# Two blocks less to fetch in each opening: sums added onto raw blocks that are kept

## The chip, the cores and the metric

The kernel runs on 1 core of one Trainium2 chip. The time is the device time of one execution in microseconds. Of the core's engines the text speaks of PE (matmuls; PEld loads its weights), DVE (element-wise arithmetic), ACT (copies, casts, functions), POOL (GpSimd) and SP; here POOL and SP mostly start transfers. Each engine works through its own list of instructions in order.

## The reference

A trunk of two layers over 528 frames (16 meta tokens and 512 inputs) of width 1024, in float32:

```
h = h + 0.5 * swiglu(rmsnorm(h, g1), w_gate1, w_up1, w_down1)      # width 2816
u = rmsnorm(h, gm);  q, k, v, a, b, g_sb, g_conv = split(u @ w_in)
h = h + (sigmoid(g_sb) * attention(q, k, v) @ w_attn_out
         + sigmoid(g_conv) * conv(a, b) @ w_conv_out) @ w_out
h = h + 0.5 * swiglu(rmsnorm(h, g2), w_gate2, w_up2, w_down2)
```

with `swiglu(x, G, U, W) = (silu(x @ G) * (x @ U)) @ W`. The conv branch begins with `a * sigmoid(b)`, so a and b form pairs of products as G and U do. A final norm closes the trunk.

## The kernel before

The weights come from memory in float32. Every block of weights (128 x 1024) is split into a high part `wh` (a cast, on ACT, L80) and a low part `wl` (the block less its high part, on DVE, L81); so are the activations (`uh`, `ul`). A product is then three matmuls: high by high, high by low, low by high. Such a prepared block is called ready.

The products of two blocks of output columns with two halves of the tokens are formed by Strassen's scheme in Winograd's form with seven instead of eight products. What lies behind a pair of column blocks (G and U at the same columns, or b and a) is: blocks `w11`, `w12`, `w21`, `w22`, and sums of them: `s1` = w11 + w12 (in the signs in which the blocks are stored), `s2` = s1 + w22, `s3` = w22 + w12, and `s4` = s1 + w21. Sums with w12 are made in flight: SP loads one block into a tile, and then POOL starts a second transfer of w12 that accumulates onto it. The other two sums are made by DVE (s2 at L283; s4 at L505, `add_w21`, in an opening). The sums of the activations have the names `sh` and `sl`.

**Openings.** At the start of a mixer's projection of a and b, and of each FFN but the first, the first two pairs of columns are worked on together, so that PE has work while the norm's scale and the activation sums are still being made. There are five openings: mixer of layer 0, second FFN of layer 0, first FFN of layer 1, mixer of layer 1, second FFN of layer 1. `OPENING` (L115) is their order of 14 units; the number is the pair (0 is called the first pair below, 1 the second). `o11` and `o21` are the blocks w11 and w21 by the unsummed activations. `w22`, `s3`, `s4` and `s2` follow with the sums of activations as these become ready.

**Preparing.** `unit` (L294) hands a ready block to PE and has the units that follow prepared two ahead in an opening (`LOOK - 1`). `prep_unit` (L254) casts, makes the low part and the DVE sums. A priority for DVE's and ACT's evictions of PE's results (`opposite`, L478; `kept`, L465) puts them ahead, and `follow` keeps a preparation behind them. All instructions of a list are then in the order in which the program was scheduled; a load that needs a tile which is still in use waits at the head of SP's list, and all loads behind it wait too.

**Tiles.** Raw blocks (`wr`, three tiles, `fetch`, L212) are taken in the order of `fetches`; `drop` gives one back. Sums in flight have tiles of their own: `s1` (two tiles) and `s3` (two in an FFN, one in the mixer); `fetch_sums` (L233) takes the next ones from the list `later_sums`. In an opening before the change:

- o11 of both pairs, o21 of both, s1 of the first pair, w22 of both: raw tiles. o11's raw block is given back when it has been split, and w11 is loaded again for s1.
- w21 of both pairs, s1 of the second pair: the `s1` tiles. o21's raw block is given back too, and w21 is loaded again.
- `WHEN` (L117) says at which units how many sums are fetched.
- o21 of the first pair has its low part made on POOL's queue (L268): ACT writes the negative high part, and a transfer adds the block.

In a quad of the main part (not an opening) the sums come as w11 (a raw block) and s1, and `DONE` (L119) says what is given back after which unit; the change does not touch it.

Of the kernel before, what the change touches and what calls it, by code (L numbers as in the profile page):

```python
# [7 lines left out]
F32 = mybir.dt.float32  # L8
# [3 lines left out]
ALU = mybir.AluOpType  # L12

P = 128
# [4 lines left out]
HALF = T // 2  # L19
# [42 lines left out]
def kernel(ctx, tc, hT, par, const, wg1, wu1, wd1, win, wao, wco, wout, wg2, wu2, wd2, out):  # L62
    nc = tc.nc
    act, dve, pool, pe = nc.scalar, nc.vector, nc.gpsimd, nc.tensor
# [32 lines left out]
    def fn(out, in_, func, **kw):  # L97
        need = SETS[func]
        if table["set"] != need:
            load = act.preload_act_table_set(need)  # L100
            for p in table["acts"]:
# [9 lines left out]
    QUAD = ("w11", "s1", "s2", "w21", "s3", "w22", "s4")  # L111
    RAW_OF = {"w11": (0, 0), "w22": (1, 1), "w12": (0, 1), "w21": (1, 0),
              "o11": (0, 0), "o21": (1, 0)}
    OPEN = ("o11", "o21")
    OPENING = (("o11", 0), ("o11", 1), ("o21", 0), ("s1", 0), ("s2", 0), ("o21", 1), ("w22", 0), ("s3", 0), ("s1", 1),  # L115
               ("s2", 1), ("s4", 0), ("s3", 1), ("w22", 1), ("s4", 1))
    WHEN = {("s2", "s1"): 1, ("s3", "w22"): 1, ("s4", "s2"): 1, ("s4", "w22"): 2}  # L117
    BLOCKS = QUAD + OPEN
    DONE = {"w11": ("w11",), "s1": (), "s2": (), "w21": (), "s3": ("s3",), "w22": ("w22",), "s4": ("s1", "w21")}  # L119

# [17 lines left out]
    units, opened = [], set()  # L138
# [36 lines left out]
    ready, raws, counted = {}, {}, set()  # L175
    quads = {"pool": None, "of": None}

    def pieces(n, block=None):

        key, src, nk = units[n]  # L180
        if nk in BLOCKS:
            wg, wu, m = src
            k, c = RAW_OF[block or nk]
            return [(4 * e, 4 * e + 4, w[m + c, :, 4 * k:4 * k + 4]) for e, w in enumerate((wg, wu))]
        return [(0, nk, src[:, :nk])]
# [4 lines left out]
    for n, (key, src, nk) in enumerate(units):  # L190
        at = key[1:]
        if nk == "w11":
            later_sums += [(n, "s1"), (n, "s3")]
            fetches += [(n, (name, *at), name) for name in ("w11", "w22", "w21")]
        elif at in opened and nk in QUAD:
            if nk == "s1" and units[n - 1][2] in OPEN:
                later_sums += [(n, "s3"), (n, "w21")]
                fetches.append((n, key, nk))
            elif nk == "s1":
                later_sums += [(n, "s1"), (n, "s3"), (n, "w21")]  # L200
            elif nk == "s2":
                fetches.append((n, ("w22", *at), "w22"))
        elif nk not in QUAD:
            fetches.append((n, key, nk))

    def load(raw, n, *blocks):
# [5 lines left out]
    def fetch(spare=None):  # L212

        while state["fetch"] < len(fetches) and (spare or state["out"] < RAW):
            n, key, block = fetches[state["fetch"]]
            state["fetch"] += 1
            if spare:
                raw = spare
            else:
                state["out"] += 1  # L220
                counted.add(key)
                raw = wpool.tile([P, 8, P], F32, tag="wr", bufs=RAW, name="wr")
            load(raw, n, *(("w11", "w12") if block == "s1" else (block,)))
            raws[key] = raw
            if spare:
                return

    def drop(key):

        del raws[key]  # L230
        state["out"] -= key in counted

    def fetch_sums(count):  # L233

        some = []
        for n, name in later_sums[state["sums"]:state["sums"] + count]:
            if units[n][0][1:3] == quads["of"]:
                some.append((n, name))
        state["sums"] += len(some)
        for n, name in some[::-1]:  # L240
            tag = "s3" if name == "s3" else "s1"
            bufs = 1 if name == "s3" and units[n][0][1] == 2 else 2
            raws[(name, *units[n][0][1:])] = quads["space"].tile([P, 8, P], F32, tag=tag, bufs=bufs, name=tag)
        for n, name in some:
            load(raws[(name, *units[n][0][1:])], n, *{"s1": ("w11", "w12"), "s3": ("w22", "w12")}.get(name, (name,)))
# [8 lines left out]
    def prep_unit():  # L254
        n = state["prep"]
        key, src, nk = units[n]
        state["prep"] += 1
        fetch()
        hi = wpool.tile([P, 8, P], F32R, tag="wh", bufs=4, name="wh")
        lo = wpool.tile([P, 8, P], F32R, tag="wl", bufs=4, name="wl")  # L260
        ready[key] = (hi, lo)
        if nk not in QUAD:
            raw, nk0, nk = raws[key], nk, 8 if nk in OPEN else nk
            if key[0] in MIXER and key[0] + str(key[2]) not in ("q0", "k0") or nk0 == "o21" and units[n - 1][2] == "o11":
                act.copy(hi[:, :nk], raw[:, :nk])  # L265
                act.activation(lo[:, :nk], raw[:, :nk], AF.Copy, scale=-1.0)
                for a, b, src in pieces(n):
                    pool.dma_start(lo[:, a:b], src.bitcast(F32R), accum_op=ALU.add)  # L268
            else:
                pair_ = split(raw[:, :nk], hi[:, :nk], lo[:, :nk])  # L270
                if state["behind"]:
                    for i, engine in zip(pair_, ("act", "dve")):
                        follow(i, engine)
            drop(key)
        else:
            at = key[1:]
            if at in opened:
                fetch_sums(WHEN.get((nk, units[n - 1][2]), 0))
            elif nk == "w11":
                fetch_sums(2)  # L280
            if nk == "s2" or nk == "s4" and at not in opened:
                x, y = raws[("s1", *at)], raws[("w22" if nk == "s2" else "w21", *at)]
                i = dve.tensor_tensor(out=x, in0=x, in1=y, op=ALU.add)  # L283
                if at in opened:
                    follow(i, "dve")
            pair_ = split(raws[("s1" if nk in ("s2", "s4") else nk, *at)], hi, lo)
            if at in opened:
                for i, engine in zip(pair_, ("act", "dve")):
                    follow(i, engine)
            for d in DONE[nk]:  # L290
                drop((d, *at))
        fetch()

    def unit(*key):  # L294
# [146 lines left out]
    def pair(ptile, sp, st, mode, of, ats, between, take, done):  # L441
# [56 lines left out]
        between(ptile(), copy)  # L498

        Bs.append(kept(As[1], False))  # L500
        G, q, E, c22 = {}, {}, {}, {}

        def add_w21(n):
            x, y = raws[("s1", *of, ats[n])], raws[("w21", *of, ats[n])]
            dve.tensor_tensor(out=x, in0=x, in1=y, op=ALU.add)  # L505

        def step(name, n):
            if (name, n) in (("w22", 0), ("s4", 0)):
                add_w21(int(name == "s4"))
            w = unit(name, *of, ats[n])  # L510
            if name == "o21":
                products(As[n], w, x(0, 1))
                (out if n else take)(n, As[n], 0, 0)
                if n:
                    keep, Bs[n], G[n] = Bs[n], ptile("pe"), ptile()
                    begin(Bs[n], keep)
            elif name == "s1":
                if not n:
                    G[n] = ptile()
                products(G[n], w, sx(0), True)  # L520
                q[n] = kept(G[n])
            elif name == "s2":
                products(Bs[n], w, sx(1))
                E[n] = ptile()
                opposite(E[n], Bs[n], q[n])
            elif name == "s3":
                products(Bs[n], w, sx(2))
                c22[n] = sp.tile([P, 2, TH], F32, tag="c22", bufs=2, name="c22")
                opposite(c22[n], Bs[n], q[n])
                take(n, c22[n], 1, 1)  # L530
            elif name == "w22":
                products(E[n], w, sx(3))
                out(n, E[n], 1, 0)
            else:
                done(n, 1)
                products(Bs[n], w, x(1, 1))
                out(n, Bs[n], 0, 1)
                done(n, 0)
# [95 lines left out]
    def ffn(l, fi, st, mode, after):  # L634
# [3 lines left out]
        with tc.tile_pool(name=f"ffn{l}{fi}", bufs=1, reuse_waits="tile") as fp, \  # L638
# [215 lines left out]
            with tc.tile_pool(name=f"quad{l}{fi}", bufs=1, reuse_waits="tile") as sp:  # L854
                quads.update(pool=sp, space=sp, of=(fi, l))
                if not first:
                    fetch_sums(2)
                (first_head if first else head)()
                m = PLAIN_FIRST
                for gi, (m0, m1) in enumerate(GROUPS):  # L860
                    while m < m1:
                        quad(sp, m)
                        m += 2
                    if gi < len(GROUPS) - 1:
                        down(gi, gi == 0 and not first)
                quads["pool"] = None
# [7 lines left out]
    def mixer(l, st, omode, after):  # L874
        last = omode == XO
        with ExitStack() as es:
# [73 lines left out]
            with tc.tile_pool(name=f"glu{l}", bufs=1, reuse_waits="tile") as glu, \  # L950
# [33 lines left out]
                quads.update(pool=glu, space=gls, of=(2, l))  # L984
                if l == 0:
                    constants(gls)
                fetch_sums(2)
                with tc.manual_schedule(engines={mybir.EngineType.PE}):
                    pair(btile, glu, st, FULL, (2, l), (0, 2), between, take, done)
                quads["pool"] = None  # L990
# [382 lines left out]
```

## Time and profile before

| | us |
|---|---|
| median of 3 runs | 2134.2 (2132.87 to 2135.08) |
| the profiled execution's own time | 2139.23 |
| span of its trace | 2137.5 |
| PE busy | 2116.6 (99%) |
| DVE busy | 1595.7 (75%) |
| ACT busy | 1170.3 (55%) |
| POOL busy | 513.2 (24%) |
| moved by DMA | 333.29 MB |

The five openings lie at about 365 to 412, 722 to 770, 1078 to 1126, 1434 to 1482 and 1778 to 1826 us of the span. A row of the timeline gives start, length, engine, line, operation, the tile written, the tiles read and, in brackets, how long the engine stood idle before it and who released it. `wr` is a raw tile, `s` an s1 or s3 tile. SPq and POOLq are the engines' issuing of transfers. In the chain of waits a row `DMA wr<-wu` runs from the issue of a transfer to its landing. A block of an FFN is two transfers of 256 KB: one from `wg` (gate) and one from `wu` (up).

### The profile page before, as it was taken

The numbers are of one execution on the slowest core, as the hardware profiler recorded it, in microseconds if no ns is written. First come the engines' busy times: TensorE is split into PE (matmuls) and PEld (weight loads), VectorE is DVE, ScalarE is ACT, GpSimd is POOL, SyncE is SP. The second block draws the span as 40 slices with busy tenths as digits, with TensorE's granted clock in tenths as the row PEclk, the third lists the DMA queues.
The fourth block names the chain that finished last, engine by engine and source line by source line (L and its number), as shares of the span: only waits on it lengthen the run. The fifth ranks groups of instructions, "written<-read, shape, count | busy, mean of one in ns | idle before, by whom it ended". The sixth has DMA issues, their size and how long they took to land.

```text
span 2137.5 us, 39987 instructions
## 1 busy us (share of the span) xinstructions
PE 2116.6 (99%) x16058; PEld 2031.3 (95%) x16058; DVE 1595.7 (75%) x2230; ACT 1170.3 (55%) x1663; POOL 513.2 (24%) x475
## 2 busy tenths in 40 slices
PE   9999999999999999999999999999999999999998
PEld 9999999999999999999999999999888888999897
DVE  6867688788876777577787676887788767867685
ACT  5434356577776645343564343565778775444354
POOL 1322321311111141313123223213212112422320
PEclk9999999999999999999999999999999999999999
DMA  7465538555578867464386655375656788765542
GB/s 228 136 167 142 144 104 229 160 135 123 128 174 178 198 175 185 120 167 119 99 204 173 167 145 142 104 223 155 143 123 140 182 186 200 186 178 143 144 109 79
DMA packets 151833, 333.29 MB, mean 156 GB/s; under 512 B 16864, under 2 KB 21088, under 8 KB 151648
## 3 DMA queue, kind: packets, MB, share of 16 engines
q1 hardware_dynamic: 110928, 235.27, 34.7%
q0 software_dynamic: 40032, 94.91, 26.2%
q8 instruction: 126, 2.06, 0.4%
q14 instruction: 59, 0.48, 0.1%
q10 hardware_dynamic: 688, 0.55, 0.1%
HBM read 324.25 MB, written 6.42 MB: 155 GB/s over the span
## 4 chain that ended last, share of the span: by engine, by line
PE 91%; DVE 4%; DMA 3%; ACT 1%; issue 1%; SPq 0%; DVEq 0%; POOL 0%; ACTq 0%; POOLq 0%
PE pb L771 15%; PE ps L771 15%; PE ps L916 13%; PE ps L311 12%; PE ps L902 10%; PE pe L311 6%; PE pb L311 5%; PE pe L771 5%; DMA wr<-wu 1%; PE z L1101 1%; DMA s<-wg 1%; PE po L1145 1%; DVE wl L81 1%; PE z L1124 1%; PE pe L462 1%; PE be L462 1%
## 5 line engine op out<-in xcount | busy, mean ns | idle before, releaser
L80 ACT CAST wh<-wr 128x1024 fp32r<-128x1024 f32 (+4 forms) x298 | 265.6, 900 | 331.4 <-PE ps L311 85.5
L81 DVE TENSOR_TENSOR wl<-wr,wh 128x1024 fp32r<-128x1024 f32 (+4 forms) x298 | 331.6, 1117 | 57.9 <-ACT wh L80 55.6
L80 ACT CAST wh<-s 128x1024 fp32r<-128x1024 f32 x171 | 179.1, 1049 | 271.6 <-DVE s L283 94.1
L81 DVE TENSOR_TENSOR wl<-s,wh 128x1024 fp32r<-128x1024 f32 x171 | 233.0, 1362 | 55.1 <-ACT wh L80 54.4
L829 POOL TENSOR_TENSOR h<-h,dt 128x528 f32<-128x528 f32 (+1 forms) x96 | 177.3, 1855 | 247.4 <-DVE dt L827 247.3
L916 PE MATMUL ps<-uh,wh 128*128 128x264 f32 (+1 forms) x664 | 207.5, 312 | 0.0
L916 PE MATMUL ps<-ul,wh 128*128 128x264 f32 (+1 forms) x664 | 203.6, 307 | 0.0
L916 PE MATMUL ps<-uh,wl 128*128 128x264 f32 (+1 forms) x664 | 203.5, 307 | 0.0
L210 POOL DMA_DIRECT2D s<-wg x81 | 71.6, 884 | 523.5 <-DMA s<-wg 290.8
L945 DVE SCALAR_TENSOR_TENSOR y<-uc,prm,y 128x528 f32<-128x528 f32 (+1 forms) x240 | 184.5, 807 | 0.5
L771 PE MATMUL ps<-ul,wh 128*128 128x264 f32 (+1 forms) x576 | 163.7, 284 | 0.0
L771 PE MATMUL pb<-sl,wh 128*128 128x264 f32 (+1 forms) x576 | 163.3, 283 | 0.0
L771 PE MATMUL ps<-uh,wl 128*128 128x264 f32 (+1 forms) x576 | 163.3, 283 | 0.0
L771 PE MATMUL pb<-sh,wl 128*128 128x264 f32 (+1 forms) x576 | 163.2, 283 | 0.0
L771 PE MATMUL pb<-sh,wh 128*128 128x264 f32 (+1 forms) x576 | 162.9, 283 | 0.0
L771 PE MATMUL ps<-uh,wh 128*128 128x264 f32 (+1 forms) x576 | 162.6, 282 | 0.0
L311 PE MATMUL ps<-ah,wh 128*128 128x264 f32 (+1 forms) x616 | 141.9, 300 | 0.0
L311 PE MATMUL ps<-al,wh 128*128 128x264 f32 (+1 forms) x616 | 141.8, 300 | 0.0
L311 PE MATMUL ps<-ah,wl 128*128 128x264 f32 (+1 forms) x616 | 141.7, 300 | 0.0
L265 ACT CAST wh<-wr 128x1024 fp32r<-128x1024 f32 x89 | 93.4, 1049 | 82.0 <-PE ps L916 28.3
L916 PEld LDWEIGHTS ps<-uh,wl 128*128 128x128 f32 x664 | 125.0, 188 | 5.9
L916 PEld LDWEIGHTS ps<-uh,wh 128*128 128x128 f32 x664 | 124.9, 188 | 5.4
(419 smaller groups left out, 6833.4 us busy)
## 6 DMA issues: line engine op xcount, KB each, us to landing
wr<-wd SPq DMA_DIRECT2D x96, 384.0 KB, 3.8
wr<-wg SPq DMA_DIRECT2D x129, 256.0 KB, 3.1
wr<-wu SPq DMA_DIRECT2D x129, 256.0 KB, 3.7
wr<-win SPq DMA_DIRECT2D x56, 512.0 KB, 3.8
wl<-win POOLq DMA_DIRECT2D x52, 512.0 KB, 7.8
s<-wg SPq DMA_DIRECT2D x87, 256.0 KB, 4.8
s<-wu SPq DMA_DIRECT2D x87, 256.0 KB, 5.6
s<-wg POOLq DMA_DIRECT2D x81, 256.0 KB, 5.5
```

What stands on the lines that cost most here:

```text
L80: i = act.copy(hi, x)
L81: return i, dve.tensor_tensor(out=lo, in0=x, in1=f(hi), op=ALU.subtract)
L210: queue.dma_start(raw[:, a:b], src, **kw)
L265: act.copy(hi[:, :nk], raw[:, :nk])
L311: pe.matmul(ps[:, c, :n], wt[:, k0 + k, :], xt[:, s:s + n], start=(k == 0 and pi == 0), stop=(k == end and pi == 2))
L462: pe.matmul(ps[:, e, :TH], wt[:, 4 * e + kk, :], xt, start=start and kk == 0 and pi == 0, stop=kk == KH - 1 and pi == 2, skip_group_check= ...
L771: pe.matmul(ps[:, e, :TH], wt[:, 4 * e + kk, :], xt, start=start and kk == 0 and pi == 0, stop=kk == 3 and pi == 2, skip_group_check=True)
L829: pool.tensor_tensor(out=tri(h[j], mode), in0=tri(h[j], mode), in1=tri(t, mode), op=ALU.add)
L902: pe.matmul(ps, wt[:, k0 + k, :], xt[:, s], start=(n == 0 and pi == 0), stop=(n == nk - 1 and pi == 2))
L916: pe.matmul(ps, wt[:, k, :], xt[:, s], start=(n == 0 and pi == 0), stop=(n == KD - 1 and pi == 2))
L945: t = dve.scalar_tensor_tensor(out=y, in0=uc[i][:, c0 + k:k + T], scalar=col(w0 + k), in1=y, op0=ALU.mult, op1=ALU.add)
L1101: pe.matmul(z[:, hh, :n], kk[r, ks], qq[r, q0:q0 + n], start=(pi == 0), stop=False, skip_group_check=True)
```

## The change

In an opening, o11's raw tile is kept: POOL adds w12 onto it, once it has been split, and it becomes s1. o21's raw block is kept until s4's sum. So w11 and w21 are loaded once instead of twice for each pair. s1 of both pairs now are in raw tiles, with w21 of the first pair in the third; w21 of the second pair and both blocks w22 are in the `s1` tiles. `fetch_sums(3)` loads the second pair's o21, the first's w22 and the first's s3 at the start, and one each follows after s3 and w22. The first pair's s3 is worked on ahead of its w22 instead of behind it. `c22`, the result of s3, gets its two tiles at the start. `WHEN` is gone.

```diff
-    OPENING = (("o11", 0), ("o11", 1), ("o21", 0), ("s1", 0), ("s2", 0), ("o21", 1), ("w22", 0), ("s3", 0), ("s1", 1),
+    OPENING = (("o11", 0), ("o11", 1), ("o21", 0), ("s1", 0), ("s2", 0), ("o21", 1), ("s3", 0), ("w22", 0), ("s1", 1),
                ("s2", 1), ("s4", 0), ("s3", 1), ("w22", 1), ("s4", 1))
-    WHEN = {("s2", "s1"): 1, ("s3", "w22"): 1, ("s4", "s2"): 1, ("s4", "w22"): 2}
...
         elif at in opened and nk in QUAD:
-            if nk == "s1" and units[n - 1][2] in OPEN:
-                later_sums += [(n, "s3"), (n, "w21")]
-                fetches.append((n, key, nk))
-            elif nk == "s1":
-                later_sums += [(n, "s1"), (n, "s3"), (n, "w21")]
-            elif nk == "s2":
-                fetches.append((n, ("w22", *at), "w22"))
-        elif nk not in QUAD:
+            if nk == "s3" and units[n - 1][2] == "o21":
+                later_sums += [(n - 1, "o21"), (n + 1, "w22"), (n, "s3")]
+            elif nk == "s3":
+                later_sums += [(n, "s3"), (n + 1, "w22")]
+        elif nk not in QUAD and (nk != "o21" or units[n - 1][2] == "o11"):
             fetches.append((n, key, nk))
...
-        for n, name in some[::-1]:
+        for n, name in some:
...
-            drop(key)
+            if nk0 in OPEN:
+                same = "s1" if nk0 == "o11" else "w21", *key[1:]
+                raws[same] = raws.pop(key)
+                if key in counted:
+                    counted.add(same)
+                if nk0 == "o11":
+                    for a, b, src in pieces(n, "w12"):
+                        pool.dma_start(raw[:, a:b], src, accum_op=ALU.add)
+            else:
+                drop(key)
         else:
             at = key[1:]
-            if at in opened:
-                fetch_sums(WHEN.get((nk, units[n - 1][2]), 0))
-            elif nk == "w11":
+            if nk == "w11":
                 fetch_sums(2)
...
-            for d in DONE[nk]:
+            for d in DONE[nk][:1] if at in opened else DONE[nk]:
                 drop((d, *at))
+            if at in opened and nk in ("w22", "s3"):
+                fetch_sums(1)
         fetch()
...
-        G, q, E, c22 = {}, {}, {}, {}
+        G, q, E, c22 = {}, {}, {}, quads["c22"]
 
         def add_w21(n):
             x, y = raws[("s1", *of, ats[n])], raws[("w21", *of, ats[n])]
             dve.tensor_tensor(out=x, in0=x, in1=y, op=ALU.add)
+            drop(("w21", *of, ats[n]))
+            fetch()
...
-                c22[n] = sp.tile([P, 2, TH], F32, tag="c22", bufs=2, name="c22")
...
-                    fetch_sums(2)
+                    quads["c22"] = [sp.tile([P, 2, TH], F32, tag="c22", bufs=2, name="c22") for _ in range(2)]
+                    fetch_sums(3)
```

The mixer's opening changes at its `fetch_sums` in the same way.

How the lists of instructions move is shown in the third opening (first FFN of layer 1); the line numbers after the change are those of the changed kernel. SP's loads, before: `s3_13321` is s3 of the first pair, `s1_13320` and `s1_13608` are w21 loaded again for the first and the second pair, `s1_13426` is w11 for the second pair's s1, `s3_13533` its s3, and `wr_13468` its w22.

```order
L210 DMA s3_13321<-wg1 128x512
L210 DMA s3_13321<-wu1 128x512
L210 DMA s1_13320<-wg1 128x512
L210 DMA s1_13320<-wu1 128x512
L210 DMA s1_13426<-wg1 128x512
L210 DMA s1_13426<-wu1 128x512
L210 DMA s3_13533<-wg1 128x512
L210 DMA s3_13533<-wu1 128x512
L210 DMA s1_13608<-wg1 128x512
L210 DMA s1_13608<-wu1 128x512
L210 DMA wr_13468<-wg1 128x512
L210 DMA wr_13468<-wu1 128x512
```

After: `s1_13291` is the second pair's o21, `s1_13292` the first pair's w22, `s3_13293` its s3, `s3_13468` the second pair's s3, `wr_13575` the first down weights, `s3_13682` the s3 of the first quad behind the opening, and `s1_13504` the second pair's w22.

```order
L206 DMA s1_13291<-wu1 128x512
L206 DMA s1_13292<-wg1 128x512
L206 DMA s1_13292<-wu1 128x512
L206 DMA s3_13293<-wg1 128x512
L206 DMA s3_13293<-wu1 128x512
L206 DMA s3_13468<-wg1 128x512
L206 DMA s3_13468<-wu1 128x512
L206 DMA wr_13575<-wd1 128x512
L206 DMA s3_13682<-wg1 128x512
L206 DMA s3_13682<-wu1 128x512
L206 DMA s1_13504<-wg1 128x512
L206 DMA s1_13504<-wu1 128x512
```

The loads of w21 and w11 are gone; the first pair's s3 stands behind o21 and w22, and the second pair's w22 is in an `s1` tile and behind down weights and the next quad's s3.

DVE in the same opening, from the first low part behind the first pair's s4 sum, before: `wl_13465` is the second pair's o21, `wl_13499` the first pair's w22, `wl_13532` its s3, `wl_13574` the second pair's s1, and L283 its s2.

```order
L81 TENSOR_TENSOR wl_13465<-wr_13261,wh_13464 128x1024
L691 TENSOR_TENSOR up_13459<-pe_13332,g_13458 128x264
L81 TENSOR_TENSOR wl_13499<-wr_13207,wh_13498 128x1024
L481 SCALAR_TENSOR_TENSOR ps_13528<-pb_13330,q_13496 128x264 x2
L81 TENSOR_TENSOR wl_13532<-s3_13321,wh_13531 128x1024
L689 TENSOR_TENSOR g_13564<-ps_13331,rstd_13383 128x264
L81 TENSOR_TENSOR wl_13574<-s1_13426,wh_13573 128x1024
L691 TENSOR_TENSOR up_13565<-ps_13331,g_13564 128x264
L689 TENSOR_TENSOR g_13601<-ps_13528,rstd_13383 128x264
L283 TENSOR_TENSOR s1_13426<-s1_13426,wr_13468 128x1024
```

After: `wl_13434` is o21, `wl_13465` the first pair's s3, `wl_13501` its w22, `wl_13540` the second pair's s1, and L286 its s2.

```order
L81 TENSOR_TENSOR wl_13434<-s1_13291,wh_13433 128x1024
L697 TENSOR_TENSOR up_13428<-pe_13306,g_13427 128x264
L81 TENSOR_TENSOR wl_13465<-s3_13293,wh_13464 128x1024
L486 SCALAR_TENSOR_TENSOR ps_13497<-pb_13304,q_13462 128x264 x2
L81 TENSOR_TENSOR wl_13501<-s1_13292,wh_13500 128x1024
L695 TENSOR_TENSOR g_13531<-ps_13305,rstd_13357 128x264
L81 TENSOR_TENSOR wl_13540<-wr_12991,wh_13539 128x1024
L697 TENSOR_TENSOR up_13532<-ps_13305,g_13531 128x264
L486 SCALAR_TENSOR_TENSOR c22_13289<-pb_13304,q_13462 128x264 x2
L695 TENSOR_TENSOR g_13569<-c22_13289,rstd_13357 128x264
L286 TENSOR_TENSOR wr_12991<-wr_12991,s1_13504 128x1024
```

s3 has changed places with w22, so the tile of w22 (`s1_13292`), which the load of the second pair's w22 (`s1_13504`) needs, comes free at the third low part of this piece instead of a tile of its own at the second.

POOL's transfers of the same opening, before: s1 of the first pair, o21's low part and s3 of the first pair.

```order
L210 DMA wr_13136<-wg1 128x512
L210 DMA wr_13136<-wu1 128x512
L268 DMA wl_13256<-wg1 128x512
L268 DMA wl_13256<-wu1 128x512
L210 DMA s3_13321<-wg1 128x512
L210 DMA s3_13321<-wu1 128x512
```

After: s1 of both pairs onto o11's tiles, then the same.

```order
L277 DMA wr_12939<-wg1 128x512
L277 DMA wr_12939<-wu1 128x512
L277 DMA wr_12991<-wg1 128x512
L277 DMA wr_12991<-wu1 128x512
L264 DMA wl_13228<-wg1 128x512
L264 DMA wl_13228<-wu1 128x512
L206 DMA s3_13293<-wg1 128x512
L206 DMA s3_13293<-wu1 128x512
```

Two transfers that stood behind o21's low part now stand ahead of it.

More of the change, by code (lines that the diff above doesn't have):

```diff
@@ L986, in mixer @@
                     constants(gls)
-                fetch_sums(2)
+                quads["c22"] = [glu.tile([P, 2, HALF], F32, tag="c22", bufs=2, name="c22") for _ in range(2)]
+                fetch_sums(3)
                 with tc.manual_schedule(engines={mybir.EngineType.PE}):
```

## The prediction

> **What bounds the kernel now.** I read the page's busy times first, then its chain, then the waits of TensorE (PE), then the busy time in the five openings. Page:
>
> ```profile
> span 2137.5 us, 39987 instructions
> PE 2116.6 (99%) x16058; PEld 2031.3 (95%) x16058; DVE 1595.7 (75%) x2230; ACT 1170.3 (55%) x1663; POOL 513.2 (24%) x475
> PE 91%; DVE 4%; DMA 3%; ACT 1%; issue 1%; SPq 0%; DVEq 0%; POOL 0%; ACTq 0%; POOLq 0%
> ```
>
> PE is busy for 2116.6 of 2137.5 us, so at most 20.9 us can be won without taking matmuls away, and the change takes none away. The waits of PE say by whom it is stopped (columns: total us, times, longest):
>
> ```profile
> PE ps L747 <- ACT wh L80: 4.9, 1, 4.9
> PE pe L462 <- DVE wl L81: 2.3, 3, 0.8
> PE pe L462 <- DVE ps L481: 1.3, 3, 0.5
> PE pe L462 <- ACT wh L80: 1.3, 2, 0.8
> PE be L462 <- DVE bs L481: 1.2, 1, 1.2
> PE bs L462 <- DVE wl L81: 0.6, 2, 0.3
> PE be L462 <- ACT bb L475: 0.5, 2, 0.3
> ```
>
> L747 is the kernel's start. L462 is the products of an opening, so the other six rows, 7.2 us, lie in the five openings. Busy time there (window, us, then PE, PEld, DVE, ACT, POOL, clock, DMA share, GB/s; the second opening, the fourth, and the sum of the five):
>
> ```profile
> 722.00:770.00 48.00, 46.28 (x376) 45.66 (x375) 37.46 (x60) 26.74 (x41) 10.81 (x14) 1.00 0.89 209
> 1434.00:1482.00 48.00, 46.31 (x371) 45.40 (x370) 40.11 (x60) 30.34 (x45) 13.80 (x16) 1.00 0.52 143
> sum 239.00, PE 231.86 PEld 227.57 DVE 194.30 ACT 144.00 POOL 63.98; mean PE 46.37 PEld 45.52 DVE 38.86 ACT 28.80 POOL 12.80
> ```
>
> 239.00 - 231.86 = 7.1 us idle, which agrees with the 7.2. The DMA engines are 0.89 busy in the FFN opening and 0.52 in the mixer's. So the time is PE's own, plus about 7 us of idle time in the openings, and this change can reach only those.
>
> A stop costs more than its row, because the pipeline of matmuls drains and fills. Second opening, where unit s2 of the second pair begins:
>
> ```profile
> 750.36 0.29 PE L462 MATMUL ps<-sl,wh 128*128 128x264 f32 x1
> 750.48 0.28 PE L462 MATMUL ps<-sh,wl 128*128 128x264 f32 x1
> 751.28 0.40 PE L462 MATMUL pe<-sh,wh 128*128 128x264 f32 x1 [0.51 <-ACT wh L80]
> 751.51 0.28 PE L462 MATMUL pe<-sl,wh 128*128 128x264 f32 x1
> 752.53 0.39 PE L462 MATMUL pe<-sh,wl 128*128 128x264 f32 x1 [0.75 <-DVE wl L81]
> ```
>
> From 750.36 to 750.48 is 0.12, the undisturbed step of a matmul. From 750.48 to 751.28 is 0.80, so 0.68 is lost where the row says 0.51; the matmul after a stop starts 0.23 later instead of 0.12. A stop costs its row + 0.17 + 0.11 = row + 0.28; the two here cost 1.58 together.
>
> **What the stop waits for.** The chain in the second opening:
>
> ```profile
> 738.90 0.42 DVE up L691
> 739.37 9.35 DMA wr<-wu
> 748.84 1.24 DVE s L283
> 750.18 1.05 ACT wh L80
> 751.26 1.23 DVE wl L81
> 758.26 0.45 DVE ps L481
> ```
>
> The second block w22 of the second pair lands at 748.72, 9.35 us after its issue; then come sum s2 (L283), the cast and the low part. DVE works in order, so the late sum also pushes L481 (758.26), on which unit s3 of that pair waits: these are the three `DVE ps L481` stops. The same load stands in the third and fifth opening's chains:
>
> ```profile
> 1096.89 8.18 DMA wr<-wu
> 1796.20 9.24 DMA wr<-wu
> ```
>
> In the fourth opening (a mixer, one s3 buffer) the second pair's s3 is loaded into the buffer that the first pair's low part frees at 1455.89:
>
> ```profile
> 1455.90 5.46 DMA s<-win
> 1462.50 5.68 DMA s<-win
> 1469.37 1.23 DVE wl L81
> ```
>
> **The change part by part.** *Forty loads of 256 KB fewer on SP's queue, the same number of accumulates on POOL's, the same instructions on PE, ACT and DVE:* no engine that bounds the time has less to do, so this is worth only what it takes off the stops. *s3 of the first pair one unit earlier:* frees the fourth opening's s3 buffer a unit, about 2.9 us, sooner (a unit is 24 matmuls at 0.12); the 1.2 stop there goes. *The loads that compete with w22's second block are gone (both w21, both w11):* it lands in less time and the stops in the FFN openings shrink. All that could go: `DVE wl` 2.3, `DVE ps` 1.3, `ACT wh` 1.3, `DVE bs` 1.2 = 6.1 us in 9 stops, so 6.1 + 9 x 0.28 = **8.6 us**. The 4.9 at the start and the last two rows have other causes, and stay.
>
> *But w22's second block is issued later.* It now takes the buffer of w22's first block and has to wait for that block's low part, which stands in DVE's order where this row stands now:
>
> ```profile
> 741.18 1.22 DVE L81 TENSOR_TENSOR wl<-s,wh 128x1024 fp32r<-128x1024 f32 x1
> 764.04 0.69 DVE L81 TENSOR_TENSOR wl<-wr,wh 128x512 fp32r<-128x512 f32 x1
> wr<-wu SPq DMA_DIRECT2D x129, 256.0 KB, 3.7
> s<-wu SPq DMA_DIRECT2D x87, 256.0 KB, 5.6
> s<-wu POOLq DMA_DIRECT2D x81, 256.0 KB, 6.8
> ```
>
> It is issued at 741.18 + 1.22 = 742.4, its second half some 0.4 later, at 742.8: three microseconds later than today's 739.37. From landing (748.72) to the third matmul (752.53) are 3.81 us; without a stop that matmul would start at 750.48 + 3 x 0.12 = 750.84, so the block must land by 747.03, which is 4.2 us after 742.8. Medians of such loads are 3.7 (raw tiles) and 5.6 (sum tiles). With 3.7 it lands at 746.5 and nothing stops; with 5.6 at 748.4, 1.4 late. Down weights and the next quad's s3 are ahead of it in the queue, so I take the middle, 4.7: 747.5, late by **0.5 in each of three FFN openings, +1.5** (bounds 0 and 4.2, or more if it is as slow as now).
>
> *Third opening: two new places.* The rows (SP, POOL, DVE, PE):
>
> ```profile
> 1079.69 0.42 SPq L210 DMA_DIRECT2D s<-wu  x1
> 1073.72 0.88 POOL L210 DMA_DIRECT2D wr<-wg  x1 [23.16 <-DVE sl L81]
> 1087.80 0.86 POOL L210 DMA_DIRECT2D s<-wg  x1 [7.42 <-DMA s<-wg]
> 1079.68 0.70 DVE L396 TENSOR_TENSOR nsum<-nsum,sq 128x528 f32<-128x528 f32 x1
> 1094.56 1.22 DVE L81 TENSOR_TENSOR wl<-wr,wh 128x1024 fp32r<-128x1024 f32 x1
> 1098.74 0.28 PE L462 MATMUL ps<-sh,wh 128*128 128x264 f32 x1
> ```
>
> The tile of s3 is now loaded behind o21's and w22's, and the first of those takes a buffer that waits for `nsum` (done at 1080.38). Three pairs of SP issues of some 0.4 a DMA put s3's second half at 1082.4 instead of 1079.69; 5.6 to landing makes 1088.0, POOL's issue some 0.7 more, 6.8 to landing 1095.5, cast 1.05, low part 1.23: 1097.9 at the earliest. Its unit now starts where w22's starts today, 1098.74. That is 0.9 of room, less than the scatter of such loads (9.24 in a row above, 3.7 in a median): lower bound 0, upper bound 1.9 + 0.9, if one load needs 3.6 more = 2.8; I take **+1.0**, nearer to the rows' medians. The sum s2 of the first pair goes behind one more low part on DVE, so the one at 1094.56, which ends at 1095.78 against a need at 1096.05 (its unit's third matmul), can stop PE for a few tenths: **+0.3** (0 to 0.7).
>
> *The accumulates onto o11's blocks* stand ahead of o21's low part on POOL. [...] By the rows: two more pairs ahead on POOL take 2 x 1.3 us, and POOL had been idle for 23.16 us before 1073.72, so they are issued as soon as o11's casts are done; I take 0 (0 to 2.6 in an opening).
>
> *Buffers held longer* (three raw tiles until the sums of the first pair): the first down weights now wait for the first pair's sum at L505, which stands ahead of the row of 741.18 on DVE; the first low part of a down block (512 wide) is the row of 764.04, so they have over 20 us, and I take 0.
>
> Sum: -8.6 + 1.5 + 1.0 + 0.3 = **-5.8**. The profiled execution took 2139.23 (span 2137.5 and 1.7 around it) and would take 2133.4; the median of the runs is 2134.2, 5.0 lower for a reason that the profile does not show, so I set the difference against the median: 2128.4.
>
> **The rivals.** *(1) The wait only moves (within 0.2%).* w22's second block takes 5.6, lands at 748.4 and stops PE by 1.4 + 0.28, today's 1.58. Then the three stops of L481 stay too, the fourth opening's 1.2 + 0.28 goes and 1.3 come in the third: 2134. Partly so, 2131.5. For it: the later issue, and 0.89 of DMA. Against: the two competitors that are gone.
>
> *(2) Slower.* The same load takes what it takes now, 8.2 to 9.35, since 0.89 of DMA stays. From 5.9 us on (748.72 - 742.8) the later issue decides. With 8.2 it lands at 751.0, 4.0 late instead of today's 748.72 - 747.03 = 1.7: +2.3, in three openings +7, less the fourth's 1.5, plus the third's 1.3: +6.8, **2141**. Against it: eight fewer loads in each opening; for it: 9.35 is what a load in this place has needed.
>
> *(3) Everything goes:* no late block, no stop in the third: 2134.2 - 8.6 = 2125.6. [...]
>
> *(4) The change does not do what it says* (the traffic of an opening doesn't fall): the order of the rows on SP excludes it but for 1 in 100.
>
> **How the numbers follow.** 0.2% is 4.3 us, about what can be told from no change here. Chances: my forecast 0.40, (3) 0.14, (1) 0.33, (2) 0.12, (4) 0.01. The forecast's own range is 2126 to 2131.5, 0.07 of it over 2129.9, where faster ends; 0.06 of (1) lies under that. Faster 0.33 + 0.14 + 0.06 = 0.53, within 0.2% 0.07 + 0.27 = 0.34, slower 0.13. The range goes from a little under (3), 2124.5, through (1) to 2136, where 0.1 of (2) is left above.
>
> **What would show it.** Right: the rows `DVE wl`, `DVE ps` and `ACT wh` at `pe L462` fall from 4.9 to under 2.5 us, `be <- DVE bs` is gone, w22's second block lands within 5 us, and the openings' PE idle time falls from 7.1 to about 3. The third opening has a short stop at s3 of the first pair. Wrong: a load of w22 of 5.6 or more; a stop at o21's first unit, behind POOL; a new wait in the units after the openings; or a changed clock.

## The result and the profile after

The changed kernel takes 2138.37 us (median of 20 runs, 2136.67 to 2142.69), the kernel before 2134.61 us in 20 runs of the same comparison (2132.87 to 2139.28). The ratio is 1.0018, with a 95% interval of 1.0012 to 1.0024: 3.8 us slower, where 5.8 us faster was forecast, and outside the range. That is just inside the 0.2% that had been called "no change", but its interval leaves out 1.

The page of the profile after (a profiled execution of 2137.33 us):

```profile
span 2135.6 us, 39935 instructions
PE 2116.3 (99%) x16058; PEld 2031.6 (95%) x16058; DVE 1597.0 (75%) x2230; ACT 1170.0 (55%) x1663; POOL 512.6 (24%) x475
DMA packets 146074, 322.80 MB, mean 151 GB/s; under 512 B 16225, under 2 KB 20449, under 8 KB 145889
```

PE does the same work, and 10.5 MB less are moved (333.29 before), so the change does what it says. The span is 1.9 us shorter than that of the first profile of before, although the median is longer; the second profiles, below, show why. What PE waits for (total us, times, longest):

```profile
PE ps L753 <- ACT wh L80: 4.8, 1, 4.8
PE ps L316 <- DVE up L697: 4.5, 3, 1.8
PE bs L467 <- DVE wl L81: 0.5, 2, 0.3
PE be L467 <- ACT bb L480: 0.5, 2, 0.3
```

Compare with the seven rows of before: all waits of FFN openings (`pe L462`) are gone, and so is the mixer's `be <- DVE bs`. One row is new: L316 is the products with the down weights, right behind an opening, and it waits three times for `up` at L697. The chain of waits, third opening:

```profile
1115.68 6.73 DMA wr<-wd
1122.79 0.63 ACT wh L80
1123.44 0.69 DVE wl L81
1124.13 0.35 DVE up L697
1124.53 2.43 PE ps L316 x12
1126.95 2.31 PE pb L316 x12
```

A load of down weights, its cast and its low part stand ahead of `up` (the product of the gate and up parts of an FFN, from which the down product takes its activations). In the second opening the same, first ACT's timeline after, then DVE's, then PE's:

```profile
766.44 0.62 ACT L80 CAST wh<-wr 128x512 fp32r<-128x512 f32 x1 [4.34 <-DMA wr<-wd]
766.96 0.42 ACT L104 ACTIVATE g<-g 128x264 f32<-128x264 f32 x1
```

```profile
762.50 0.43 DVE L697 TENSOR_TENSOR up<-c,g 128x264 f32<-128x264 f32 x1
767.09 0.69 DVE L81 TENSOR_TENSOR wl<-wr,wh 128x512 fp32r<-128x512 f32 x1 [4.16 <-ACT wh L80]
767.70 0.43 DVE L697 TENSOR_TENSOR up<-ps,g 128x264 f32<-128x264 f32 x1
```

```profile
764.84 0.40 PE L316 MATMUL ps<-ah,wh 128*128 128x264 f32 x2
768.18 0.51 PE L316 MATMUL ps<-ah,wh 128*128 128x264 f32 x2 [1.74 <-DVE up L697]
```

and SP's, after (four loads in one row):

```profile
759.42 8.71 SPq L206 DMA_DIRECT2D wr<-wd  x4
```

The three first down products begin together (12 matmuls of each in turn). The second of them writes the accumulator that `up` still has to read. `up` needs the activated `g` of ACT (L104). That instruction had its input from DVE at 762.6, but it stands behind the third down block's cast on ACT's list, and `up` itself stands behind that block's low part on DVE's list. Each engine works in order, so the late load holds both: ACT idles 4.34 us and DVE 4.16. The block's load is issued at 759.42, 5.4 us before the first down product (764.84). Before, in the second profile (below), it went out 7.9 us before (SP's timeline, then PE's):

```profile
756.83 0.33 SPq L210 DMA_DIRECT2D wr<-wd  x1
```

```profile
764.72 0.40 PE L311 MATMUL ps<-ah,wh 128*128 128x264 f32 x2
```

Why later: before, the tile for the third down block came from the second pair's w22, whose low part is one unit ahead of the last. After, it comes from the second pair's s1, whose last reader is the low part of the last unit, s4 (it ends at 759.40, and the load goes out at 759.42). 2.5 us are lost there. The load also takes longer, here the same load after and in the second profile of before:

```profile
wr<-wd SPq DMA_DIRECT2D x1, 256.0 KB, 6.9
```

```profile
wr<-wd SPq DMA_DIRECT2D x1, 256.0 KB, 3.9
```

So 3.0 us of its lateness are in the landing, more than the 2.5 in the issue. After, it stands behind a pair of loads into a sum tile (755.90 and 756.27 us) that in the second profile of before comes behind it (759.83 and 760.21); no run tests whether that is why it is slower.

The three stops cost 4.5 + 3 x 0.28 = 5.3 us. And there is a second price. Busy time in stretches of 3.41 us around two of the stops, the second of each pair right behind the first (window, us, PE, PEld, DVE, ACT, POOL, granted clock, DMA, GB/s):

```profile
766.90:770.31 3.41, 2.13 (x17) 2.13 (x18) 2.09 (x4) 1.51 (x4) 0.00 (x0) 1.00 1.12 246
770.31:773.72 3.41, 3.41 (x30) 3.41 (x29) 1.74 (x3) 1.18 (x3) 0.00 (x0) 1.00 0.37 105
1121.88:1125.29 3.41, 1.61 (x14) 1.40 (x13) 1.15 (x3) 1.58 (x3) 0.00 (x0) 1.00 1.11 260
1125.29:1128.71 3.42, 3.42 (x18) 3.42 (x17) 2.23 (x5) 1.57 (x3) 0.00 (x0) 0.50 0.84 197
```

Behind the stop of 1.74 us the granted clock stays 1.00; behind that of 1.80 it is halved for 3.4 us, and the 24 matmuls at the end of the chain above take 2.43 + 2.31 instead of 24 x 0.12 = 2.9 us. Some 1.7 us, half of the stretch, are lost by it.

### The profile page after: what moved, and what is told of

The parts are those of the page before. It is cut to its first block, busy times and chain, and to the rows that moved or that the text cites. A ratio compares the mean times of both kernels' runs of the same rounds, so it can differ in the third digit from the quotient of the medians.

```text
span 2135.6 us, 39935 instructions
## 1 busy us (share of the span) xinstructions
PE 2116.3 (99%) x16058; PEld 2031.6 (95%) x16058; DVE 1597.0 (75%) x2230; ACT 1170.0 (55%) x1663; POOL 512.6 (24%) x475
## 4 chain that ended last, share of the span: by engine, by line
PE 96%; DVE 2%; DMA 1%; ACT 1%; issue 0%; DVEq 0%; ACTq 0%
PE pb L777 15%; PE ps L777 15%; PE ps L923 13%; PE ps L316 12%; PE ps L909 10%; PE pe L316 6%; PE pb L316 5%; PE pe L777 5%; PE ps L467 2%; PE pb L467 1%; PE pe L467 1%; PE bs L467 1%; PE z L1109 1%; PE po L1153 1%; DMA wr<-wd 1%; PE z L1132 1%
## 5 line engine op out<-in xcount | busy, mean ns | idle before, releaser
L316 PE MATMUL ps<-ah,wh 128*128 128x264 f32 (+1 forms) x616 | 142.6, 301 | 4.5 <-DVE up L697 4.5
L316 PE MATMUL ps<-ah,wl 128*128 128x264 f32 (+1 forms) x616 | 142.2, 301 | 0.0
L316 PE MATMUL ps<-al,wh 128*128 128x264 f32 (+1 forms) x616 | 142.1, 300 | 0.0
```

Source lines behind the costliest of these rows:

```text
L316: pe.matmul(ps[:, c, :n], wt[:, k0 + k, :], xt[:, s:s + n], start=(k == 0 and pi == 0), stop=(k == end and pi == 2))
```

## The experiments

**Was the first profile typical?** Both kernels, unchanged, were profiled once more. Before:

> The kernel before, unchanged, for a second profile. Theory A (the first profile of the kernel before, 2139.2 us, was an unlucky execution, since its timed runs have a median of 2134.6): this profile has a span of about 2133 us, and the waits of PE in the openings on the weights' low and high parts and on the evictions (6.1 us in nine stops in the first profile) are about half or less. Theory B (the profile is typical and the stops are always there): the span is about 2137 us and these waits are again 5 to 7 us.

2132.87 us, span 2131.1, 6.4 us less than the first profile of the same kernel. The waits of its openings, but for two rows that all these kernels share (`bs <- DVE wl`, `be <- ACT bb`):

```profile
PE pe L462 <- DVE ps L481: 0.9, 2, 0.5
PE pe L462 <- DVE wl L81: 0.4, 1, 0.4
PE be L462 <- DVE bs L481: 0.2, 1, 0.2
```

Busy time in the second opening and in all five, and the load of w22's second half in the second opening (transfers of 738 to 750 us):

```profile
722.00:770.00 48.00, 48.00 (x396) 48.00 (x395) 38.11 (x61) 28.07 (x43) 12.19 (x14) 1.00 0.92 226
sum 239.00, PE 236.39 PEld 231.69 DVE 191.49 ACT 146.42 POOL 67.29; mean PE 47.28 PEld 46.34 DVE 38.30 ACT 29.28 POOL 13.46
```

```profile
wr<-wu SPq DMA_DIRECT2D x1, 256.0 KB, 6.9
```

1.5 us in four stops instead of 6.1 in nine; 1.5 + 4 x 0.28 = 2.6 instead of 8.6. PE idles 239.00 - 236.39 = 2.6 us in the five openings, not 7.1. The load of w22's second half took 6.9 us, not 9.35, and in that opening PE did not idle at all (48.00 of 48.00). Theory A holds: the profile on which the forecast was built was an unlucky execution. This one is at the other end: 2132.87 is the fastest of the 20 timed runs of the kernel before. An execution at their median, 2134.6, would have some 2.6 + 1.7 = 4.3 us of such stops (an estimate from these two numbers). The changed kernel:

> The changed kernel, unchanged, for a second profile. In its first profile PE waits 4.5 us in three stops for the activation parts of the first down products behind an FFN opening, and behind one of these stops the granted clock is halved for 3.4 us. Expected if these are the cause of the loss: again three stops of 1 to 2 us, and zero to three stretches of half clock of 3.4 us, each directly behind one of them; the time is about 2136.5 + 1.7 for each such stretch. If they were chance: the stops are gone or elsewhere.

2140.14 us, span 2138.4. Its waits, and the stops in PE's timeline:

```profile
PE ps L316 <- DVE up L697: 5.3, 3, 2.0
PE pb L467 <- DVE ps L486: 0.2, 1, 0.2
```

```profile
768.16 0.51 PE L316 MATMUL ps<-ah,wh 128*128 128x264 f32 x2 [1.35 <-DVE up L697]
1125.11 0.51 PE L316 MATMUL ps<-ah,wh 128*128 128x264 f32 x2 [1.94 <-DVE up L697]
1824.61 0.50 PE L316 MATMUL ps<-ah,wh 128*128 128x512 f32 x1 [1.98 <-DVE up L697]
```

The same three stops; half clock behind the second and third (two stretches of 3.4 us in the records; the granted clock is 0.67 over 1124.6 to 1128.6 us and 0.62 over 1824.8 to 1828.8), none behind that of 1.35 (1.00 over 768.2 to 771.2). So the stops are not chance, and the time is what two such stretches were expected to make of it (2136.5 + 2 x 1.7 = 2139.9). Among the 20 timed runs, the five with a mean clock of 0.999 took 2136.7 to 2137.8 us, and the six with 0.996 or 0.997 took 2139.1 to 2142.7.

**One more raw tile.** The changed kernel, with an extra tile in FFN openings:

```diff
             drop(("w21", *of, ats[n]))
             fetch()
+            if n == 0 and of[0] != 2:
+                fetch(sp.tile([P, 8, P], F32, tag="more", bufs=1, name="more"))
```

> The changed kernel with one more raw tile in the three FFN openings, taken at the sum of s4 for the first pair; so each of the first down blocks loads one tile earlier and none waits for the last unit of the opening. Theory A (the third down block's load waits for the raw tile of the second pair's s1, which is given back only at the last unit): the three stops behind the openings go, 4.5 us by the rows and 5.5 with their starts, and the half clock behind them; 2130 to 2132 us, a ratio of 0.998 to 0.999 to the kernel before. Theory B (the loss comes from elsewhere, say from the clock or from DVE's order): still 2137 to 2139 us.

2130.91 us (11 runs, 2130.03 to 2132.13), ratio 0.9981 (0.9972 to 0.9990). Its waits and DVE's list at the same place:

```profile
PE pb L467 <- DVE ps L486: 0.3, 1, 0.3
```

```profile
762.90 0.68 DVE L81 TENSOR_TENSOR wl<-wr,wh 128x512 fp32r<-128x512 f32 x1
763.50 0.42 DVE L699 TENSOR_TENSOR up<-ps,g 128x264 f32<-128x264 f32 x1
```

The third down block's load now goes out 8.5 us earlier (SP's timeline):

```profile
750.95 0.33 SPq L206 DMA_DIRECT2D wr<-wd  x1
```

Its low part still stands ahead of `up`, but the block is there, and `up` runs at 763.50 instead of 767.70. No stop behind the openings is left. Theory A holds, and this kernel beats both.

The other way round, holding a tile in the kernel before:

```diff
-            for d in DONE[nk]:
+            late = at in opened and at[0] != 2 and at[2] == 2
+            for d in () if late and nk == "w22" else DONE[nk] + (("w22",) if late and nk == "s4" else ()):
                 drop((d, *at))
```

> The kernel before, but in the three FFN openings the raw tile of the second pair's w22 is given back with the last unit instead of its own. Theory A (a raw tile held to the last unit makes the third down block late): three stops of PE at the down products as in the changed kernel, 1 to 2 us each, some with half clock behind them; +4 to +10 us. Theory B (the release of that tile does not matter): the same time as the kernel before, within 2 us.

2135.12 us, ratio 1.0004 (0.9995 to 1.0012). This edit moved the load only in the text of the program: in the second opening the third load's issue (758.53) and the first down product (766.43) are 7.9 us apart as before, since a load waits for the last reader of its tile (w22's low part), not for the place where the program gives it back. So the run tells nothing about the theory, only that.

**Is it the lateness, or the place on DVE's list?** Preparation two ahead instead of three to the end of the opening:

```diff
-            if (name, n) == ("s3", 1):
+            if (name, n) == ("s3", 1) and of[0] == 2:
                 state["look"] = LOOK
             step(name, n)
+        state["look"] = LOOK
```

> The changed kernel, with preparation two units ahead instead of three until the FFN openings have ended, so that the third down block is prepared one unit later; its load and its tile are as in the changed kernel. Theory A1 (the load of the third down block is late, and its low part stands on DVE ahead of the activation parts that the first down products need): the low part goes behind these parts, the three stops of 4.5 to 5.3 us go, and the time is 2130 to 2133 us, as with the further tile, though the load comes just as late. Theory A2 (the products themselves wait for the late block): the stops stay, moved to the third down block, 2136 us or more.

2135.37 us, ratio 1.0007 (0.9998 to 1.0016; one of the 11 timed runs took 7332 us, which nothing in the other ten explains). The wait row and the stop in the second opening:

```profile
PE pe L316 <- ACT wh L80: 3.3, 3, 1.3
```

```profile
769.35 0.51 PE L316 MATMUL pe<-ah,wh 128*128 128x264 f32 x2 [0.84 <-ACT wh L80]
```

The waits for `up` are gone, as A1 said, but new ones of 3.3 us for a down block's high part take their place, as A2 said. The time lies between A1's 2130 to 2133 and A2's 2136. Then the changed kernel with one small reader more on s1's tile:

```diff
+            if at in opened and at[0] != 2 and at[2] == 2 and nk == "s4":
+                i = dve.tensor_copy(quads["space"].tile([P, 1], F32, tag="held", bufs=1, name="held"), raws[("s1", *at)][:, 0, :1])
+                tc.add_manual_dep(i.ins, pair_[1].ins.name, NOSYNC, reason="held to here")
             for d in DONE[nk][:1] if at in opened else DONE[nk]:
```

> The changed kernel, with one more small reader of the second pair's s1 tile (a copy of one element a partition on DVE, behind the low part and two more instructions of DVE), so that the third down block's load is issued about 1.4 us later still. The list of DVE now has the activation parts of the first down products ahead of the third down block's low part. Theory A1 (only the place on DVE's list costs): no stop behind the openings in spite of the later load, 2131 to 2134 us. Theory A2 (the lateness of the load costs): each stop grows by 1.4 us and all three are followed by half clock, 3 x 1.4 + 3 x 1.7 over the changed kernel's fastest runs, 2144 us or more.

2135.26 us, ratio 1.0004 (0.9995 to 1.0013). Its waits and DVE's list, second opening:

```profile
PE pb L319 <- ACT wh L80: 2.3, 3, 1.3
```

```profile
763.28 0.43 DVE L700 TENSOR_TENSOR up<-ps,g 128x264 f32<-128x264 f32 x1 [0.15 <-ACT g L104]
768.47 0.69 DVE L81 TENSOR_TENSOR wl<-wr,wh 128x512 fp32r<-128x512 f32 x1 [4.76 <-ACT wh L80]
```

The load goes out 1.4 us later (4.0 us ahead of the first down product instead of 5.4), `up` and the ACT instruction that it needs now stand ahead, and the stops become shorter, not longer: 2.3 us in three, the longest 1.3. A2's 2144 is excluded, and A1's 2131 to 2134 is missed by a little. Both parts are true: the place on the lists decides what stops and for how long, and a late third block stops its own product in any case, because that begins only 24 matmuls (2.9 us) behind the first. Of what was tried, only an earlier load takes all of it away.

**Are the saved loads worth anything?** The changed kernel with eight loads of 256 KB put back into each FFN opening, into a tile that nobody reads:

```diff
+            if at in opened and at[0] != 2 and nk in ("s1", "s2"):
+                again = quads["space"].tile([P, 8, P], F32, tag="again", bufs=1, name="again")
+                i = dve.tensor_copy(again[:, :, :1], f(hi)[:, :, :1])
+                tc.add_manual_dep(i.ins, pair_[1].ins.name, NOSYNC, reason="from here")
+                for a, b, src in pieces(n, "w11" if nk == "s1" else "w21"):
+                    nc.sync.dma_start(again[:, a:b], src)
```

> The changed kernel, with eight loads of 256 KB in each FFN opening that fetch w11 and w21 again into a tile that nobody reads, started at the low parts of s1 and s2 of both pairs (as many bytes as the change had saved). In the changed kernel the second half of w22's second block landed 3.2 us after its issue, in the two profiles of the kernel before 6.9 and 9.35. Theory A (the loads that are gone had made it slow): 5 to 9 us to landing, and stops at the second pair's s2 or s3 come back beside those behind the openings; 2 to 6 us slower than the changed kernel, 2140 to 2144. Theory B (its new place on the list made it fast): 3 to 4 us, and the same time as the changed kernel, 2137 to 2140.

2145.05 us (4 runs), ratio 1.0045 (1.0030 to 1.0061). First the transfer row of the second half of w22's second block in the changed kernel, then this run's waits and the same row (the 3.2 expected above is the median of this load and that of s3's second half):

```profile
s<-wu SPq DMA_DIRECT2D x1, 256.0 KB, 3.4
```

```profile
PE ps L322 <- DVE up L703: 6.2, 3, 3.1
PE pb L473 <- DVE ps L492: 2.0, 1, 2.0
PE pe L473 <- DVE wl L81: 0.9, 2, 0.6
PE ps L473 <- DVE wl L81: 0.8, 2, 0.5
```

```profile
s<-wu SPq DMA_DIRECT2D x1, 256.0 KB, 4.6
```

With the bytes back the landing takes 4.6 us instead of 3.4 (a little under the 5 to 9 expected, and far from the 6.9 and 9.35 of the kernel before), 3.7 us of stops are back inside the openings, and those behind them grow; the time goes up by 6.7, not 2 to 6. So the bytes cost time, but they explain only a part of the slow landing before, where the load also had another place on SP's list. The copies that start these loads cost DVE four short instructions an opening (0.17 us for the one at 744.30), so not quite all of the 6.7 is the loads'. The extra tile without the change:

```diff
             dve.tensor_tensor(out=x, in0=x, in1=y, op=ALU.add)
+            if n == 0 and of[0] != 2:
+                fetch(sp.tile([P, 8, P], F32, tag="more", bufs=1, name="more"))
```

> The kernel before with the same further tile in the three FFN openings, and nothing else of the change. Theory A (the gain of the kernels with the further tile comes from the loads saved, the tile only mends what the change broke): the first down block loads earlier, among the loads that make w22's second block late, so the same as the kernel before or up to 3 us slower, 2134 to 2138. Theory B (the tile is the gain): 2130 to 2132.

2135.22 us, ratio 1.0002 (0.9993 to 1.0011), with

```profile
PE pe L462 <- DVE ps L481: 1.2, 3, 0.4
PE pe L462 <- DVE wl L81: 1.0, 3, 0.4
```

So the tile alone is worth nothing, and the gain of the kernel with both needs the change. That the saved loads are what counts in it fits the run with the loads put back; the loads' new places on the lists were not tested apart from them.

**The order of units.** The kernel with the extra tile, with w22 ahead of s3 again for the first pair (and the loads of the second pair's w22 and s3 listed in that order):

```diff
-    ("o21", 1), ("s3", 0), ("w22", 0), ("s1", 1),
+    ("o21", 1), ("w22", 0), ("s3", 0), ("s1", 1),
...
-                later_sums += [(n - 1, "o21"), (n + 1, "w22"), (n, "s3")]
+                later_sums += [(n - 1, "o21"), (n, "w22"), (n + 1, "s3")]
```

> The kernel with the further raw tile, with the first pair's w22 ahead of its s3 again, as before the change. Theory A (the order of units is worth the stop at the second pair's s3 in the mixer of layer 1, and costs a stop in the third opening): the mixer's stop comes back with 0.4 to 1.4 us and the third opening's 0.4 us goes: the same as the kernel with the further tile or up to 1 us slower, 2130.5 to 2132. Theory B (the order carries the gain): 2133 us or more.

2130.23 us (2129.71 to 2131.20), ratio 0.9981 (0.9972 to 0.9990), and of the kernels here its five openings are the busiest (sum of the windows):

```profile
sum 239.00, PE 237.93 PEld 233.16 DVE 191.50 ACT 145.92 POOL 59.82; mean PE 47.59 PEld 46.63 DVE 38.30 ACT 29.18 POOL 11.96
```

The third opening's stop is gone, and the mixer's did not come back. So the new order of units is worth nothing that these runs show. Both kernels with the extra tile have the ratio 0.9981, 4 us under the kernel before.

**Do these losses account for the times?** Lost time of seven profiled executions: the wait rows in and behind the openings (without the two shared ones), 0.28 for each stop, 1.7 for each stretch of half clock ahead of the kernel's tail.

| kernel | rows, stops, stretches | lost | span | span less lost |
|---|---|---|---|---|
| before, first profile | 6.1, 9, 0 | 8.6 | 2137.5 | 2128.9 |
| before, second profile | 1.5, 4, 0 | 2.6 | 2131.1 | 2128.5 |
| changed, first profile | 4.5, 3, 1 | 7.0 | 2135.6 | 2128.6 |
| changed, second profile | 5.5, 4, 2 | 10.0 | 2138.4 | 2128.4 |
| changed, loads put back | 9.9, 8, 3 | 17.2 | 2145.2 | 2128.0 |
| changed, extra tile | 0.3, 1, 0 | 0.6 | 2129.4 | 2128.8 |
| the same, old order of units | 0, 0, 0 | 0 | 2127.9 | 2127.9 |

The mean granted clock of these executions falls with the stretches: 0.999 without one, 0.998 with one, 0.997 with two, 0.996 with three. In these seven everything else agrees within 1 us. The same count leaves 2128.4 for the preparation two ahead and for the extra tile alone, 2129.2 for the further small reader, and 2130.2 for the tile held in the kernel before. So stops and half clock account for most of what tells these kernels apart; up to 2.3 us between two executions stay unexplained.

## Why the prediction was wrong

**What bounds the kernel, and what a stop costs:** right. PE is the bound, a stop costs its row + 0.28, and the table holds with it. (The two stops that the prediction priced together at 1.58 cost 0.51 + 0.75 + 2 x 0.28 = 1.82 by that rule; only rival (1) used the 1.58.)

**All that could go, 8.6 us:** the nine stops went indeed, all of them. But 8.6 was the price in one execution, 2139.23 us, of which the profile was taken; the runs shown had a median of 2134.2, and an execution at 2132.87 has only 2.6 us of such stops. The step that failed is the one that "set the difference against the median", for "a reason that the profile does not show". Between the two profiles, 6.0 of the 6.4 us are these very stops. With 2.6 in place of 8.6 the same sum reads -2.6 + 1.5 + 1.0 + 0.3 = +0.2, and with the 4.3 estimated for a median execution -1.5; both are no change.

**The fourth opening's 1.2:** the stop went, but not by the step that was named, s3 worked on one unit earlier. The kernel with the old order of units has no stop there either, and the second profile of before has 0.2.

**w22's second block, +1.5:** its issue was foreseen to within 0.4 us (742.8; it was 742.47), but it lands in 3.4 us, not 4.7, and stops nothing: 0. The saved loads are a part of the reason (4.6 us with the bytes put back). So rivals (1) and (2), which hung on this landing, both fall; a slower result came, but by another mechanism.

**Third opening, +1.0 and +0.3:** 0 in the first profile after, one stop of 0.2 us by its row in the second (0.5 with its starts). Inside the bounds, and too high.

**Buffers held longer, 0:** this is the step that cost the forecast its sign. It looked at the first down block, which does have over 20 us. The third needs the last raw tile to come free, and that is held to the last unit's low part; its load lands at 766.34 in the second opening, after the first down product has begun at 764.84, and until then ACT and DVE hold back what the second one needs. Measured: 5.3 us in the first profile and 6.1 in the second (5.3 + 3 x 0.28), and 1.7 for each stretch of half clock. The prediction did name "a new wait in the units after the openings" and "a changed clock" as what would show it wrong, but gave neither a price. Three signs that it named for being right came true (the rows at `pe L462`, `be <- DVE bs`, and the landing of w22), and yet the time rose: all three look inside the openings.

With both put right, by the two profiles of after and the second of before: 7.0 - 2.6 = +4.4 and 10.0 - 2.6 = +7.4, against spans of +4.5 and +7.3. The medians differ by 3.8, which is less, as a median execution of before has more stops than this second profile (4.3 us by the estimate above).

## What to carry to other kernels

When tiles of a small pool are held longer, follow every one of them to its next user, the last to come free above all, and look at what stands behind that user's preparation on each in-order engine: the engine waits for the load, and work that had long been ready waits with it, as here for 4.34 us on ACT and 4.16 on DVE. Before a stall seen in a profile is counted as a gain, compare that execution's own time with the median of the runs; where they differ by more than the gain, take a second profile first.

## What the runs showed of the hardware

Three stops of PE of 1.80, 1.94 and 1.98 us (by the wait rows above) were each followed by 3.4 us of half clock, while stops of 1.74 and 1.35 us, and one of 1.01 behind the fifth opening in the first profile of the changed kernel, were not. With the 1.7 us that such a stretch loses, the stop of 1.98 us cost some 3.7, nearly twice its length (an estimate from these two numbers). What decides between the stop of 1.74 us, where the granted clock stayed at 1.00, and that of 1.80, behind which it was 0.50, the runs do not show.

The same load, w22's second half in the second opening of the kernel before, took 9.35 us in one execution and 6.9 in another, with 0.89 and 0.92 of the DMA engines busy in that opening. In the changed kernel, with eight loads of 256 KB fewer in that opening, it took 3.4, with 0.75 busy.
